# First layer of a four-layer decoder trunk on one core: VectorE's queue in another order, and the query and gate projections in turn

## The chip, the core and the metric

One core of a Trainium2 chip runs the whole program. The time is device microseconds of one execution on that core. The number of the kernel before is the median of 3 runs, 585.58 us (585.5 to 586.86). The engines are named as in the profile: PE is TensorE (matmuls; PEld its weight loads), DVE is VectorE, ACT is ScalarE, POOL is GpSimd, and SP issues most of the DMAs. Each engine takes its own instructions in order; between engines, semaphores order the work.

## The reference

The input x has 256 positions of 1024 numbers. Four layers follow each other, each `h = h + rms_norm(mixer(rms_norm(h)))`, with four different mixers. Only the first one is touched here, a sparse attention with 16 query heads in 4 groups that share keys and values:

```
q, kc, vc, ks, vs, kw, vw, gl, z = split_cols(u @ w_in, A_SPLITS)
kcmp, vcmp = compress(kc, ...), compress(vc, ...)          # 15 blocks of 32 positions
p_c = masked_softmax(q @ kcmp - slopes * dist, dist >= 0)  # compressed branch, 15 columns
p_s = masked_softmax(q @ ks  - slopes * dist, dist >= 0)   # selected branch: here all 4 blocks
p_w = masked_softmax(q @ kw  - slopes * dist, mask)        # window branch
o = gates[0] * (p_c @ vcmp) + gates[1] * (p_s @ vs) + gates[2] * (p_w @ vw)
return (o * silu(z)) @ w_out
```

With 256 positions the selected branch and the window branch see the same causal columns. The gates are sigmoids of `gl`.

## The kernel before, in words

Every float32 product with a weight matrix is made of three matmuls on fp32r halves. A weight tile is loaded as `raw` (by SP, 512 KB, five buffers), ACT makes its high half `whi` (line 129), DVE its low half `wlo` (line 72, a subtraction), and PE multiplies high by high, high by low and low by high (weights by activations, lines 222 to 224 in `mm3`). `push_proj` puts one projection of 256 columns into the queue `fq` as 16 steps of three matmuls each, and hands the finished PSUM tile `mm` (three buffers) to a function `use`.

The first layer's attention runs as 8 units (`nsa_unit`) of two query heads each, two units to a group of four heads. PE's order is that of the source (it is scheduled by hand), and in this layer DVE's too; ACT's order is chosen by the tile scheduler from priorities. `nsa_order` lists the pieces of the units: `first` and `second` of unit p (the scores of the first and of the second half of the positions), the two transpositions of unit p-1 (`trans`, line 328, into the two PSUM buffers `pt`), then `finish` (the rest of the scores) and `pvs` of unit p-1 (the products with the values, lines 344, 347 and 875). Ahead of each even unit stands `cmp_front` (scores of the compressed branch, line 783), in each odd unit `cmp_back` (their transposition, line 811). Between two pieces `fill` pops steps of waiting projections from `fq`, two at first and then one, so that PE has work while the other engines make the softmax.

What DVE does for a unit:

- `softmax` (line 321): one operation adds mask and scores, writes `P` and accumulates the maximum `mxa` (a second, short instruction reads it out). It frees the score tile `S` (two PSUM buffers), and ACT's exponential (line 323) follows. These are called the maxima here.
- `scale` (lines 849 to 859), called the weighting: reciprocal of the sums, times the gate, and eight multiplications of parts of `P`. PE's transposition of the unit (line 328) reads what they write.
- In each even unit the compressed branch: a reduction of its scores (line 787), five small operations that follow from one another (789 to 796), ACT's exponential (797), and five more (`cmp_weights`, 801 to 806).
- The low halves of weights (line 72), called by `low_parts` and by `push_proj`, and what `later` has put off: the low half of the queries (line 681), the gate's `zw` (430), its product with the output (381) and the low half of that (390). `later(n, f)` runs f once n more steps have been popped.

The order of the compressed branch and of the weighting comes from these calls:

```
cmp_front(g)   # lines 787 to 797 at once, ahead of the unit's first maxima
first()        # scores_of(0, (0, 1)), then CHALF (801 to 806), then SCALE of unit p-1
trans_first()  # for the last unit: SCALE, then its first transposition
```

The projections in `fq` are the queries of groups 1 to 3 (group 0 is done earlier) and then the four parts of z. `need(g)` pops steps until the queries of group g have been ready for six steps.

## Time and profile before

| what | value |
|---|---|
| median of 3 runs | 585.58 us (585.5 to 586.86) |
| the profiled execution, its time | 586.66 us |
| its span in the trace | 584.9 us |
| PE / DVE / ACT / POOL busy | 561.1 / 420.6 / 335.4 / 41.8 us |
| mean granted TensorE clock | 0.99 |
| scores of the first unit begin | 68.6 us of the span |
| output projection of the first layer begins | 168.3 us |

The profiled execution took 586.66 us, 1.08 us more than the median of the runs. Its span is 1.8 us shorter than its own time; that much lies around the span. Times inside the trace count from the span's start. The ends of matmuls are modelled and overlap the next ones, so a PE that is shown busy is not at its peak; its gaps are seen from the starts of its instructions and from the view of the waits. A granted clock of 1.00 stands for 2.4 GHz, 0.5 for 1.2 GHz; a stretch with a number between them had both.

### The profile page before, as it was taken

To read this page: it belongs to the slowest core of one execution; us is meant where nothing else is said; L and a number is where in the kernel's file an instruction comes from. 1 tells how busy PE (TensorE), PEld (TensorE's weight loads), DVE (VectorE), ACT (ScalarE), POOL (GpSimd) and SP (SyncE) were. 2 spreads that over 40 slices of the span, in tenths; PEclk is the share of its full clock that TensorE was granted. 3 is DMA by queue.
4 is the path that set the end of the run, shared out by engine and by line. 5 is a ranking of instruction groups with operands and counts; after the bars stand their busy time and mean duration, and the time that the engine had idled before them with its cause. 6 is when DMAs were issued, how large, how long until landed. Compare 5 with 4: busy or idle time off the path is not lost.

```text
span 584.9 us, 10456 instructions
## 1 busy us (share of the span) xinstructions
PE 561.1 (96%) x3930; PEld 498.2 (85%) x3930; DVE 420.6 (72%) x927; ACT 335.4 (57%) x719; POOL 41.8 (7%) x89
## 2 busy tenths in 40 slices
PE   7999988988899999999999999999999999999995
PEld 6997877866688789999988789999987898998984
DVE  5883788788837887777984877668648778888632
ACT  6743777787723475766752475558524755666410
POOL 1900000000100100000420100000001000000000
PEclk9999989998999999999999999999999999999999
DMA  9764632333315577444342468543525683332012
GB/s 295 254 241 165 232 111 79 108 101 106 121 24 228 180 271 269 145 146 145 109 149 104 156 232 307 162 146 115 153 99 171 226 316 124 131 114 73 2 37 72
DMA packets 27779, 90.96 MB, mean 155 GB/s; under 512 B 4560, under 2 KB 5200, under 8 KB 27728
## 3 DMA queue, kind: packets, MB, share of 16 engines
q1 hardware_dynamic: 26144, 86.09, 43.4%
q10 hardware_dynamic: 1584, 4.20, 2.2%
q8 instruction: 31, 0.51, 0.4%
q14 instruction: 20, 0.16, 0.1%
HBM read 89.22 MB, written 1.05 MB: 154 GB/s over the span
## 4 chain that ended last, share of the span: by engine, by line
PE 81%; DVE 8%; issue 4%; ACT 3%; DMA 2%; POOL 1%; POOLq 0%; DVEq 0%; ACTq 0%; SPq 0%
PE mm L222 15%; PE mm L223 14%; PE mm L224 14%; PE mm L289 6%; PE mm L288 6%; PE mm L287 6%; PE pt L328 4%; PE S L338 3%; DVE wlo L72 3%; PE o L344 2%; ACT whi L129 2%; DMA raw<-in_a_t_dram 1%; PE o L692 1%; PE pt L210 1%; PE mm L519 1%
## 5 line engine op out<-in xcount | busy, mean ns | idle before, releaser
L222 PE MATMUL mm<-uth,whi 128*128 128x256 f32 x736 | 218.6, 297 | 0.0
L72 DVE TENSOR_TENSOR wlo<-raw,whi 128x1024 fp32r<-128x1024 f32 (+1 forms) x153 | 182.0, 1205 | 41.8 <-ACT whi L129 41.3
L224 PE MATMUL mm<-uth,wlo 128*128 128x256 f32 x736 | 208.7, 284 | 2.1 <-DVE wlo L72 2.1
L223 PE MATMUL mm<-utl,whi 128*128 128x256 f32 x736 | 208.7, 284 | 0.0
L129 ACT ACTIVATE whi<-raw 128x1024 fp32r<-128x1024 f32 (+1 forms) x153 | 157.0, 1044 | 67.4 <-PE mm L223 33.4
L222 PEld LDWEIGHTS mm<-uth,whi 128*128 128x128 f32 x736 | 141.4, 192 | 14.1 <-issue 13.3
L224 PEld LDWEIGHTS mm<-uth,wlo 128*128 128x128 f32 x736 | 141.4, 192 | 2.3 <-DVE wlo L72 2.3
L223 PEld LDWEIGHTS mm<-utl,whi 128*128 128x128 f32 x736 | 141.6, 192 | 0.8
L287 PE MATMUL mm<-whi,qT 128*128 128x512 f32 x128 | 50.4, 394 | 0.0
L288 PE MATMUL mm<-whi,kT 128*128 128x512 f32 x128 | 49.9, 390 | 0.0
L289 PE MATMUL mm<-wlo,qT 128*128 128x512 f32 x128 | 49.9, 390 | 0.0
L287 PE MATMUL mm<-whi,uth 128*128 128x512 f32 (+1 forms) x112 | 42.5, 380 | 0.0
L289 PE MATMUL mm<-wlo,uth 128*128 128x512 f32 (+1 forms) x112 | 42.1, 376 | 0.0
L288 PE MATMUL mm<-whi,utl 128*128 128x512 f32 (+1 forms) x112 | 42.0, 375 | 0.0
L328 PE MATMUL pt<-ident,P 128*128 128x128 f32 x180 | 28.9, 290 | 5.9 <-DVE P L858 4.5
L321 DVE CUSTOM_DVE_ANT_0 P<-S,mask 128x128 f32<-128x128 f32 (+1 forms) x96 | 29.1, 353 | 7.2 <-PE S L834 4.9
L452 ACT ACTIVATE junk<-mm 128x512 bf16<-128x512 f32 x16 | 9.5, 595 | 42.7 <-PE mm L289 42.7
L323 ACT ACTIVATE P<-P,mxa 128x128 f32<-128x128 f32 (+1 forms) x64 | 28.4, 446 | 6.5 <-DVE mxa L321 6.5
L168 ACT ACTIVATE PT<-pt 128x384 f32<-128x384 f32 x58 | 26.1, 483 | 8.1 <-PE pt L328 7.9
L328 PEld LDWEIGHTS pt<-ident,P 128*128 128x128 f32 x180 | 21.3, 146 | 8.9 <-DVE P L858 3.5
L289 PEld LDWEIGHTS mm<-wlo,qT 128*128 128x128 f32 x128 | 24.0, 188 | 5.1
L288 PEld LDWEIGHTS mm<-whi,kT 128*128 128x128 f32 x128 | 24.1, 188 | 4.7
(207 smaller groups left out, 757.8 us busy)
## 6 DMA issues: line engine op xcount, KB each, us to landing
raw<-in_a_t_dram SPq DMA_DIRECT2D x24, 512.0 KB, 4.4
raw<-in_b_t_dram SPq DMA_DIRECT2D x24, 512.0 KB, 4.8
raw<-in_d_t_dram SPq DMA_DIRECT2D x24, 512.0 KB, 4.5
raw<-in_c_t_dram SPq DMA_DIRECT2D x20, 512.0 KB, 4.9
raw<-in_w_dram SPq DMA_DIRECT2D x8, 512.0 KB, 4.5
raw<-in_a_o_dram SPq DMA_DIRECT2D x8, 512.0 KB, 3.4
raw<-in_b_v_dram SPq DMA_DIRECT2D x8, 512.0 KB, 5.8
raw<-in_b_o_dram SPq DMA_DIRECT2D x8, 512.0 KB, 3.5
```

What stands on the lines that cost most here:

```text
L72: lo_of = (POOL if on_pool else DVE).tensor_tensor(lo, t, hi.bitcast(F32), op=OP.subtract)
L129: ACT.activation(hi, t, AF.Copy)
L168: ACT.activation(dst, src, AF.Copy)
L222: PE.matmul(o, sh, mh, start=first, stop=False)
L223: PE.matmul(o, sh, ml, start=False, stop=False)
L224: PE.matmul(o, sl, mh, start=False, stop=last)
L287: PE.matmul(o, sh, wh[:, j, c0:c1], start=k == 0, stop=False)
L288: PE.matmul(o, sl, wh[:, j, c0:c1], start=False, stop=False)
L289: PE.matmul(o, sh, wl[:, j, c0:c1], start=False, stop=k == 7)
L321: DVE.tensor_tensor_reduce(out=P[:, c0:c1], in0=S, in1=mask[:, c0:c1], scale=-slope, scalar=BIG, op0=OP.add, op1=OP.min, accum_out=mx)
L323: ACT.activation(P[:, c0:c1], P[:, c0:c1], AF.Exp, bias=mx, scale=-1.0, accum_out=l)
L328: PE.transpose(pt[:, i, :], P[:, i * 128:(i + 1) * 128], ident)
```

## The change

Five edits, all in the first layer's attention or in helpers that act otherwise only there:

- The small operations of the compressed branch become two lists of calls in `CHALF`. The first list (lines 789 to 797 of before) runs in `first`, behind the unit's first maxima, in turn with the weighting of unit p-1 (`mixed`); the second (801 to 806) runs in `second`, behind its maxima.
- `scale` returns a list of calls, which `mixed` alternates with the others. For the last unit it is called two pieces ahead of the transposition.
- The projections are pushed as queries 1, z 0, queries 2, z 1, queries 3, z 2, z 3, and the weight tiles are loaded in that order.
- `push_proj` makes the low half of the next weight tile at the first step of a tile and no longer at the third.
- The low half of the queries and the gate's `rest` are put off by 5 and 6 steps and no longer by 3. The high half of the queries gets an early priority on ACT, the gate's tanh loses its late one, and `overdue` runs whatever is due, not only the head of its list.

```diff
@@ -57,7 +57,7 @@
     add("a_t", *range(8))
     add("a_t", 8, 9)
     add("w1", *range(8), split=False)
-    add("a_t", *range(10, 24))
+    add("a_t", 10, 11, 16, 17, 12, 13, 18, 19, 14, 15, 20, 21, 22, 23)
     add("a_o", *range(8))
     for n in "bcd":
         add(n + "_v", *range(8))
@@ -88,8 +88,12 @@
             f()
 
     def overdue(everything=False):
-        while waiting and (everything or waiting[0][0] <= plan["count"]):
-            waiting.popleft()[1]()
+        due = [w for w in waiting if everything or w[0] <= plan["count"]]
+        for w in due:
+            waiting.remove(w)
+            w[1]()
+        if due:
+            overdue(everything)
 
     def advance(most=len(seq)):
         while True:
@@ -257,7 +261,7 @@
         def step(c, k):
             if c == 0 and k == 0:
                 t["o"] = ps.tile([128, 2, 256], F32, name="mm", bufs=NMM)
-            for i, at in ((idx[c], 0), (idx[c] + 1, 2)):
+            for i, at in ((idx[c], 0), (idx[c] + 1, 0)):
                 if k == at and i in low:
                     low.pop(i)()
             wh, wl = parts[idx[c]]
@@ -355,8 +359,8 @@
             self.oT = big.tile([128, 8, 256], F32, name="oT")
             self.ready = 0
 
-        def push(self):
-            for i in range(4):
+        def push(self, *which):
+            for i in which or range(4):
                 push_proj(lambda z, i=i: self.have_z(i, z))
 
         def have_z(self, i, z):
@@ -364,7 +368,7 @@
                 self.w[i] = w
                 self.go()
 
-            with tc.high_priority(offset=LATEZ):
+            with tc.high_priority(offset=0 if st["own"] else LATEZ):
                 self.silu(z, got)
 
         def have_o(self, p):
@@ -430,7 +434,7 @@
             DVE.scalar_tensor_tensor(w, w, 1.0, z, op0=OP.add, op1=OP.mult)
             got(w)
 
-        later(3, rest)
+        later(6, rest)
 
     def out_proj(g, l):
         last = l == 3
@@ -677,8 +681,9 @@
             r, other = HALF[j], HALF[1 - j]
             hs = slice(4 * g + j, 4 * g + j + 3, 2)
             hi, sc = t["q"][r, hs, :], cq[r, 2 * g:2 * g + 1]
-            ACT.activation(hi, o[r], AF.Copy, scale=sc)
-            later(3, lambda r=r, other=other, hs=hs, hi=hi, sc=sc: DVE.scalar_tensor_tensor(
+            with tc.high_priority(offset=EARLY):
+                ACT.activation(hi, o[r], AF.Copy, scale=sc)
+            later(5, lambda r=r, other=other, hs=hs, hi=hi, sc=sc: DVE.scalar_tensor_tensor(
                 t["q"][other, hs, :], o[r], sc, hi.bitcast(F32), op0=OP.mult, op1=OP.subtract))
         ready[g] = plan["count"]
 
@@ -759,8 +764,11 @@
         for f in steps[4 * q:4 * q + 4]:
             fq.append(f)
             pop()
+    ga = Gate(0.5, silu_tanh)
     for g in range(1, 4):
         push_proj(lambda o, g=g: keep_q(o, g))
+        ga.push(g - 1)
+    ga.push(3)
     for _ in range(9):
         pop()
     hidden_t()
@@ -769,8 +777,6 @@
     second_layer()
     qT = t["q"]
 
-    ga = Gate(0.5, silu_tanh)
-    ga.push()
     CS, PTC, CHALF, SCALE = {}, {}, [], []
 
     def cmp_front(g):
@@ -786,24 +792,31 @@
         two = sc[:, 0:256].rearrange("p (a s n) -> p a n s", s=2, n=16)[:, :, 0:15, :]
         DVE.tensor_reduce(out=cs.rearrange("p b a n -> p (b a) n"), in_=two, axis=AX.X, op=OP.add)
         pairs = cs.rearrange("p b (c j) n -> p (b c) j n", j=2)
-        DVE.tensor_tensor(pairs, pairs, dcmp.rearrange("p b c n -> p (b c) n")[:, :, None, :]
-                          .to_broadcast([128, 4, 2, 15]), op=OP.add)
-        DVE.tensor_tensor(cs, cs, slc[:, g, None, :, None].to_broadcast([128, 2, 4, 15]), op=OP.mult)
         cs8 = cs.rearrange("p b a n -> p (b a) n")
         cm, cl = small(8, "cm", 2), small(8, "cl", 2)
-        DVE.tensor_reduce(out=cm, in_=cs8, axis=AX.X, op=OP.max)
-        DVE.tensor_scalar(cm, cm, -1e20, None, op0=OP.max)
-        DVE.tensor_tensor(cs8, cs8, cm[:, :, None].to_broadcast([128, 8, 15]), op=OP.subtract)
-        ACT.activation(cs, cs, AF.Exp)
-        CHALF.append(lambda: cmp_weights(g, cs, cs8, cl))
-
-    def cmp_weights(g, cs, cs8, cl):
-        DVE.tensor_reduce(out=cl, in_=cs8, axis=AX.X, op=OP.add)
-        DVE.tensor_scalar(cl, cl, 1e-30, None, op0=OP.max)
-        DVE.reciprocal(cl, cl)
-        DVE.tensor_tensor(cl.rearrange("p (b a) -> p b a", b=2), cl.rearrange("p (b a) -> p b a", b=2),
-                          gate[:, :, 4 * g:4 * g + 4], op=OP.mult)
-        DVE.tensor_tensor(cs8, cs8, cl[:, :, None].to_broadcast([128, 8, 15]), op=OP.mult)
+        cl2 = cl.rearrange("p (b a) -> p b a", b=2)
+        CHALF.append([
+            lambda: DVE.tensor_tensor(pairs, pairs, dcmp.rearrange("p b c n -> p (b c) n")[:, :, None, :]
+                                      .to_broadcast([128, 4, 2, 15]), op=OP.add),
+            lambda: DVE.tensor_tensor(cs, cs, slc[:, g, None, :, None].to_broadcast([128, 2, 4, 15]), op=OP.mult),
+            lambda: DVE.tensor_reduce(out=cm, in_=cs8, axis=AX.X, op=OP.max),
+            lambda: DVE.tensor_scalar(cm, cm, -1e20, None, op0=OP.max),
+            lambda: DVE.tensor_tensor(cs8, cs8, cm[:, :, None].to_broadcast([128, 8, 15]), op=OP.subtract),
+            lambda: ACT.activation(cs, cs, AF.Exp)])
+        CHALF.append([
+            lambda: DVE.tensor_reduce(out=cl, in_=cs8, axis=AX.X, op=OP.add),
+            lambda: DVE.tensor_scalar(cl, cl, 1e-30, None, op0=OP.max),
+            lambda: DVE.reciprocal(cl, cl),
+            lambda: DVE.tensor_tensor(cl2, cl2, gate[:, :, 4 * g:4 * g + 4], op=OP.mult),
+            lambda: DVE.tensor_tensor(cs8, cs8, cl[:, :, None].to_broadcast([128, 8, 15]), op=OP.mult)])
+
+    def mixed(*lists):
+
+        lists = [deque(x) for x in lists]
+        while any(lists):
+            for x in lists:
+                if x:
+                    x.popleft()()
 
     def cmp_back(g):
         ptc = ps.tile([128, 4, 128], F32, name="pt", bufs=2)
@@ -842,21 +855,21 @@
         def finish():
             scores_of(1, (1,))
             low_parts(1)
-            SCALE.append(scale)
+            SCALE.append(scale())
 
         def scale():
             l = t["l"]
-            DVE.reciprocal(l, l)
             gv = bass.AP(tensor=gate.tensor, offset=gate.offset + 16 + 2 * p,
                          ap=[list(gate.ap[0]), [1, 2], [16, 2], [48, 2]])
-            DVE.tensor_tensor(l.rearrange("p (j r b) -> p j r b", j=2, r=2),
-                              l.rearrange("p (j r b) -> p j r b", j=2, r=2), gv, op=OP.mult)
+            l4 = l.rearrange("p (j r b) -> p j r b", j=2, r=2)
+            ops = [lambda: DVE.reciprocal(l, l), lambda: DVE.tensor_tensor(l4, l4, gv, op=OP.mult)]
             for br in range(2):
                 for j in range(2):
                     x = (j * 2 + br) * 2
-                    P = t["P"][j, br]
-                    DVE.tensor_scalar(P[:, 0:128], P[:, 0:128], l[:, x:x + 1], None, op0=OP.mult)
-                    DVE.tensor_scalar(P[:, 128:384], P[:, 128:384], l[:, x + 1:x + 2], None, op0=OP.mult)
+                    for b in range(2):
+                        P = t["P"][j, br][:, 128 * b:128 * b + 128 * (b + 1)]
+                        ops.append(lambda P=P, x=x + b: DVE.tensor_scalar(P, P, l[:, x:x + 1], None, op0=OP.mult))
+            return ops
 
         def trans(br):
             t["PT", br] = [transpose_p(t["P"][j, br], "a") for j in range(2)]
@@ -878,25 +891,20 @@
 
         def first():
             scores_of(0, (0, 1))
-            for rest in (CHALF, SCALE):
-                if rest:
-                    rest.pop()()
+            mixed(*(x.pop(0) for x in (SCALE, CHALF) if x))
 
         def second():
             scores_of(1, (0,))
+            if CHALF:
+                mixed(CHALF.pop(0))
             low_parts(1)
 
-        def trans_first():
-            if SCALE:
-                SCALE.pop()()
-            trans(0)
-
         front = [first, second, finish]
-        back = [trans_first, lambda: trans(1), pvs]
+        back = [lambda: trans(0), lambda: trans(1), pvs]
         return front, back
 
     def nsa_order():
-        units = [nsa_unit(p) for p in range(8)] + [([lambda: None] * 3, None)]
+        units = [nsa_unit(p) for p in range(8)] + [([lambda: mixed(SCALE.pop()), *[lambda: None] * 2], None)]
         order = []
         for p in range(9):
             f, b = units[p][0], units[p - 1][1] if p else [lambda: None] * 3
```

How the instructions move, at three places of DVE's queue (line numbers of the changed kernel are 4 to 14 higher; PE's queue stays the same but for which projection a step belongs to, two steps more ahead of the last group's compressed scores and two fewer later).

DVE at the start of an even unit, the third group of heads (`cs`, `cm` and `cl` belong to the compressed branch, `la` and `P` to the weighting, `mxa` to the maxima), before:

```order
L787 TENSOR_REDUCE cs<-S 128x120
L789 TENSOR_TENSOR cs<-cs,dcmp 128x120
...
L796 TENSOR_TENSOR cs<-cs,cm 128x120
L321 ISA P,mxa<-S,mask 128x128
L321 ISA mxa 128x1
...
L801 TENSOR_REDUCE cl<-cs 128x8
...
L806 TENSOR_TENSOR cs<-cs,cl 128x120
L849 RECIPROCAL la<-la 128x8
L852 TENSOR_TENSOR la<-la,gate 128x8
L858 TENSOR_SCALAR P<-P,la 128x128
```

and now:

```order
L793 TENSOR_REDUCE cs<-S 128x120
L325 ISA P,mxa<-S,mask 128x128
...
L865 RECIPROCAL la<-la 128x8
L799 TENSOR_TENSOR cs<-cs,dcmp 128x120
L865 TENSOR_TENSOR la<-la,gate 128x8
L801 TENSOR_TENSOR cs<-cs,slc 128x120
L871 TENSOR_SCALAR P<-P,la 128x128
L802 TENSOR_REDUCE cm<-cs 128x8
L871 TENSOR_SCALAR P<-P,la 128x256
...
L325 ISA P,mxa<-S,mask 128x256
...
L807 TENSOR_REDUCE cl<-cs 128x8
```

The first maxima now follow the reduction at once, the weighting alternates with the first five operations of the compressed branch, and the last five come behind the next maxima.

DVE where the units begin (`hk` and `hv`, the hidden layer of the compression, are the copies into `P` and `zw`), before:

```order
L681 SCALAR_TENSOR_TENSOR qT<-mm,cq,qT 64x2x256 x2
L719 COPY P<-pt 128x120
L722 COPY zw<-pt 128x240 x2
L72 TENSOR_TENSOR wlo<-raw,whi 128x1024
L734 SCALAR_TENSOR_TENSOR kc<-S,kc 128x4x15
L742 TENSOR_TENSOR v<-o,bm 60x256 x4
L787 TENSOR_REDUCE cs<-S 128x120
```

and now:

```order
L686 SCALAR_TENSOR_TENSOR qT<-mm,cq,qT 64x2x256 x2
L72 TENSOR_TENSOR wlo<-raw,whi 128x1024
L724 COPY P<-pt 128x120
L727 COPY zw<-pt 128x240 x2
L739 SCALAR_TENSOR_TENSOR kc<-S,kc 128x4x15
L747 TENSOR_TENSOR v<-o,bm 60x256 x4
L793 TENSOR_REDUCE cs<-S 128x120
L72 TENSOR_TENSOR wlo<-raw,whi 128x1024
L325 ISA P,mxa<-S,mask 128x128
```

One low half now runs ahead of the copies of the hidden layer, another ahead of the first maxima.

DVE at the last unit (`zw`, `oT` and `kT` belong to the gate and its halves), before:

```order
L321 ISA P,mxa<-S,mask 128x256
L321 ISA mxa 128x1
L72 TENSOR_TENSOR wlo<-raw,whi 128x1024
L430 SCALAR_TENSOR_TENSOR zw<-zw,mm 128x512
...
L381 SCALAR_TENSOR_TENSOR oT<-oT,zw 128x512
L390 TENSOR_TENSOR kT<-oT,qT 128x512 x2
L849 RECIPROCAL la<-la 128x8
...
L858 TENSOR_SCALAR P<-P,la 128x128
```

and now:

```order
L325 ISA P,mxa<-S,mask 128x256
L325 ISA mxa 128x1
L72 TENSOR_TENSOR wlo<-raw,whi 128x1024
...
L865 RECIPROCAL la<-la 128x8
L865 TENSOR_TENSOR la<-la,gate 128x8
L871 TENSOR_SCALAR P<-P,la 128x128
...
L434 SCALAR_TENSOR_TENSOR zw<-zw,mm 128x512
```

The weighting of the last unit now stands ahead of the gate's operations.

## Rows read from the trace of the kernel before

**Rows 1.** The page, part 1: busy time, share, instructions.

```profile
PE 561.1 (96%) x3930; PEld 498.2 (85%) x3930; DVE 420.6 (72%) x927; ACT 335.4 (57%) x719; POOL 41.8 (7%) x89
```

**Rows 2.** Busy time by stretch: its length, each engine, granted clock, DMA.

```profile
68.60:91.80 23.20, 19.99 (x146) 18.00 (x145) 19.32 (x66) 17.06 (x46) 0.00 (x0) 0.93 0.36 114
91.80:114.40 22.60, 21.13 (x170) 17.90 (x169) 18.76 (x72) 16.41 (x50) 0.00 (x0) 1.00 0.28 94
114.40:134.60 20.20, 17.48 (x136) 13.88 (x134) 18.05 (x70) 16.88 (x54) 0.00 (x0) 1.00 0.33 105
134.60:155.20 20.60, 17.88 (x130) 14.64 (x129) 16.98 (x71) 15.63 (x49) 1.05 (x3) 0.92 0.33 106
155.20:168.30 13.10, 11.45 (x83) 9.60 (x81) 5.43 (x20) 5.96 (x12) 0.53 (x2) 0.87 0.14 46
```

**Rows 3.** The same view, three stretches with a low granted clock.

```profile
78.00:82.00 4.00, 4.00 (x22) 3.96 (x22) 3.94 (x17) 3.15 (x10) 0.00 (x0) 0.57 0.71 217
139.00:144.00 5.00, 3.93 (x21) 3.76 (x21) 4.42 (x17) 3.17 (x8) 0.00 (x0) 0.66 0.01 3
160.00:165.00 5.00, 5.00 (x33) 3.54 (x31) 0.64 (x2) 1.19 (x3) 0.00 (x0) 0.66 0.01 2
```

**Rows 4.** Waits of PE, 68.6 to 168.3: total us, times, longest.

```profile
PE pt L328 <- DVE P L858: 4.5, 4, 1.7
PE S L833 <- DVE mxa L321: 3.5, 4, 1.1
PE mm L224 <- DVE wlo L72: 2.1, 1, 2.1
PE pt L328 <- ACT PT L168: 1.1, 3, 0.4
```

**Rows 5.** DVE timeline, unit 6: start, us, line, operation [idle before].

```profile
135.99 0.28 DVE L789 TENSOR_TENSOR cs<-cs,dcmp 128x120 f32<-128x120 f32 x1
136.31 0.28 DVE L791 TENSOR_TENSOR cs<-cs,slc 128x120 f32<-128x120 f32 x1
...
137.34 0.28 DVE L321 CUSTOM_DVE_ANT_0 P<-S,mask 128x128 f32<-128x128 f32 x1
...
137.55 0.28 DVE L321 CUSTOM_DVE_ANT_0 P<-S,mask 128x128 f32<-128x128 f32 x1
...
138.18 0.27 DVE L801 TENSOR_REDUCE cl<-cs 128x8 f32<-128x120 f32 x1
...
139.34 0.19 DVE L849 RECIPROCAL la<-la 128x8 f32<-128x8 f32 x1
...
139.77 0.29 DVE L858 TENSOR_SCALAR P<-P,la 128x128 f32<-128x128 f32 x1
```

**Rows 6.** PE timeline of unit 6, and the last transposition.

```profile
137.99 0.47 PE L833 MATMUL S<-kT,qT 128*128 128x512 f32 x1 [1.12 <-DVE mxa L321]
...
140.11 1.59 PE L328 MATMUL pt<-ident,P 128*128 128x128 f32 x6 [1.07 <-DVE P L858]
...
158.55 1.07 PE L328 MATMUL pt<-ident,P 128*128 128x128 f32 x6 [1.65 <-DVE P L858]
```

**Rows 7.** PE timeline, units 0 and 1.

```profile
72.54 0.47 PE L833 MATMUL S<-kT,qT 128*128 128x512 f32 x1 [0.77 <-DVE mxa L321]
...
77.37 0.39 PE L224 MATMUL mm<-uth,wlo 128*128 128x256 f32 x1 [2.12 <-DVE wlo L72]
```

**Rows 8.** DVE timeline, 72 to 79.

```profile
74.55 1.52 DVE L681 SCALAR_TENSOR_TENSOR qT<-mm,cq,qT 64x512 fp32r<-64x512 f32 x2
76.09 1.22 DVE L72 TENSOR_TENSOR wlo<-raw,whi 128x1024 fp32r<-128x1024 f32 x1
```

**Rows 9.** DVE timeline at the last unit.

```profile
155.13 0.68 DVE L430 SCALAR_TENSOR_TENSOR zw<-zw,mm 128x512 f32<-128x512 f32 x1
...
158.12 0.29 DVE L858 TENSOR_SCALAR P<-P,la 128x128 f32<-128x128 f32 x1
```

**Rows 10.** ACT groups by shape, 68.6 to 168.3.

```profile
L129 ACT ACTIVATE whi<-raw 128x1024 fp32r<-128x1024 f32 x18 | 19.0, 1054 | 3.2 <-DMA raw<-in_a_o_dram 1.9 <-DMA raw<-in_a_t_dram 0.7
...
L680 ACT ACTIVATE qT<-mm,cq 64x512 fp32r<-64x512 f32 x6 | 4.1, 680 | 1.3 <-PE mm L224 1.3
...
L427 ACT ACTIVATE zw<-mm 128x512 f32<-128x512 f32 x3 | 1.8, 597 | 0.1
```

## The prediction

> **What bounds the kernel now.** I read the page's busy times first: PE is shown busy for 561.1 of 584.9 us [rows 1], so on the whole the kernel is bound by TensorE, and a change on VectorE can only be worth the time in which PE waits. The change touches the first layer's attention, so the next view is the busy time by stretch, cut at the scores of each group of heads [rows 2]. From 68.6 to 168.3 us, five stretches of 23.2, 22.6, 20.2, 20.6 and 13.1 us, PE has most of its gaps, and DVE is busy for 19.3, 18.8, 18.1 and 17.0 us of the first four: the two engines hold each other up. ACT has 15.6 to 17.1 us there. Outside these 99.7 us the order of the work is unchanged, so what is won here is kept, and what is lost too.
>
> Third, who keeps PE waiting there [rows 4]: transpositions wait for weighted P, 4.5 us in four waits; scores wait for the maxima that free a score tile, 3.5 us in four; one projection waits 2.1 us for a low half of weights; transpositions wait 1.1 us for ACT to empty a `pt` buffer. Together 11.2 us. Fourth, the granted clock: three stretches stand at 0.57 to 0.66 [rows 3], each right behind one of the longest waits: 2.12 us at 77.37 [rows 7], 1.12 and 1.07 us at 137.99 and 140.11, and 1.65 us at 158.55 [rows 6]. At 1.00 less the granted share, the last two lose 5 x 0.34 = 1.7 us of full-clock time each, and the first 4 x 0.43 = 1.7 us.
>
> Last, DVE's timeline in unit 6 [rows 5] says why PE waits. Five operations of the compressed branch run from 135.99 to 137.34, then the maxima, then from 138.18 five more, and only at 139.34 the weighting. PE's wait of 1.12 us ends with the maxima and that of 1.07 us with the first weighted P [rows 6]. Nobody needs the compressed branch that early: its transposition comes a unit later.
>
> **The change, part by part.** The sum goes against the profiled execution's own 586.66 us; the median of the runs lies 1.08 us below that, and I take the gain from the median.
>
> (a) Maxima ahead of the compressed branch. They start 137.34 - 135.99 = 1.35 us earlier [rows 5], more than any of the four waits for them (at most 1.12 us). In the even units 2, 4 and 6 these waits go: 3.5 - 0.77 = 2.7 us. In unit 0 it stays: a low half now stands ahead of those maxima, 1.22 us [rows 8] in place of 1.35 us, so the 0.77 us [rows 7] is not counted. Bounds: 1.1 us (if only the wait listed at 137.99 goes) and 3.5 us. I take **-2.7 us**.
>
> (b) Weighting in units 2, 4 and 6. Five operations (138.18 to 139.34, 1.16 us [rows 5]) leave the place ahead of it. Five others come into it, one after each operation of the weighting. Operations that depend on each other start 0.32 us apart (135.99 to 136.31), independent ones of the same length 0.21 us (137.34 to 137.55) [rows 5], so a chain that alternates with another one should hide about 0.1 us at each link. From the end of the maxima to the first weighted part were 139.77 + 0.29 - 138.18 = 1.9 us; now it is a reciprocal, two small operations of the branch, the gate and one multiplication, about 0.9 us as an estimate from these spacings. PE arrives 1.1 us earlier too, and then is paced by the second and later parts, which have an operation of the branch between each two. Of the 4.5 - 1.65 = 2.85 us [rows 4, 6] I take half, **-1.4 us**; bounds 0 and 2.85 us.
>
> (c) The last weighting stood behind the gate's operations, which start at 155.13, and its first part came at 158.12 [rows 9]; PE waited 1.65 us [rows 6]. It now stands ahead of them and two filling pieces ahead of its transposition: **-1.65 us**; bounds 0.8 us (should ACT's last exponentials come late) and 1.65 us.
>
> (d) The low half for which PE waits at 77.37 stood behind the query's 1.52 us and took 1.22 us [rows 8]. It is now issued a whole tile ahead. The 2.12 us [rows 7] go, but not for nothing. The low half that now precedes the copies of the hidden layer holds up the second layer of the compression by up to 1.22 us on PE, less the time the copies took ahead of it: I take 0.7 us. And the maxima that free the score tile for unit 1 still stand behind queries 1 and a low half, so PE stops there instead, a step later. I take **-1.0 us**; bounds +1.2 us (the whole of the copies' delay, nothing won) and -2.1 us.
>
> (e) DVE's own length. Some 6 hidden links of 0.11 us in each of three groups make 18 x 0.11 = 2.0 us of DVE time, in stretches of which DVE fills 82 to 89% [rows 2]. About half should reach PE in the odd units, which wait on the maxima at the end of this queue: **-1.0 us**; bounds 0 and 2.0 us. Queries and z in turn move work and take none away. Queries 3 now come just ahead of the compressed scores of group 3. Their low half, 1.52 us, stands behind maxima and a low half of weights (0.8 + 1.22 us), 3.5 us in all, and PE has about as much to do in between (the products with the values and three steps). That cover just holds; without it, up to 1.5 us.
>
> (f) The clock. The two later stretches follow waits that (a) to (c) shorten. Of their 3.4 us [rows 3] I take half, **-1.7 us**; bounds 0 and 5.1 us (with the first).
>
> (g) Next late is ACT. With PE earlier, transpositions meet `pt` buffers that ACT has not emptied, because one whi of 1054 ns or a pair of queries of 680 ns each [rows 10] is in front. Now 1.1 us [rows 4]; I add **+1.2 us**, bounds 0 and 3 us.
>
> The sum is -2.7 - 1.4 - 1.65 - 1.0 - 1.0 - 1.7 + 1.2 = -8.25 us, about -8.3: 578.4 us against the profiled execution, and **577.3 us** for the median.
>
> **A rule that speaks against (b) and (e).** The rows say that an independent operation starts 0.21 us after one of 0.28 us, and a dependent one after 0.32 us [rows 5]. The Trainium skill, "VectorE: DVE Perf Modes", section "The DRAIN you can't avoid", says that the next operation does not start until the pipe is empty, whether or not a semaphore stands between, and its table for kernel authors advises against chaining for speed. By that rule alternating hides nothing. The trace disagrees for operations that do not wait for each other: 0.21 us is less than the operation's own length. I go by the rows.
>
> **The rivals.**
>
> DVE stays the bound (22%). Only the waits in which DVE did plainly misplaced work go: (a) and (c), 4.35 us. The rest of DVE's queue is as full as before, and PE, arriving earlier, waits for the second and later weighted parts. For it: DVE's 82 to 89% [rows 2]. Against it: DVE too has idle time, waiting for scores that PE would deliver earlier. 585.58 - 4.35 = **581.2 us**.
>
> Alternating hides nothing (6%). DVE keeps its 2.0 us in the three groups: (e) falls away and (b) loses about as much again as the links in front of the first weighted parts, 0.3 us in each unit. 577.3 + 1.0 + 0.9 = **579.2 us**. This is what the skill's section named above would have.
>
> The full clock (10%). All three slow stretches vanish and (b) comes whole: (f) is 5.1 in place of 1.7 us, (b) 2.85 in place of 1.4. 577.3 - 3.4 - 1.45 = **572.5 us**. For it: each stretch has its wait right in front. Against it: the first wait moves by a step and does not go.
>
> ACT becomes the bound, and it is slower (6%). ACT's queue holds whi, query halves and tanh ahead of the copies that empty `pt`, and the change gives the queries an early priority and the tanh no late one. If in each of the 8 units a transposition waits for one whi more (8 x 1.05 = 8.4 us), and in six for a pair of queries or a tanh (3 x 1.36 + 3 x 0.6 = 5.9 us), that is 14.3 us against 9.45 us won in (a) to (f): **590.4 us**. It decides from 9.45 / 8 = 1.2 us for each unit. For it: ACT's 17 us in the first stretches. Against it: only 1.1 us of such waits now [rows 4], and 3.3 to 6.2 us without work in each of the four stretches [rows 2].
>
> Nothing is won (6%): PE waits as long at the next operation of DVE's queue, **585.6 us**.
>
> **How the numbers follow.** The forecast has 50%: 577.3 us, with 575 to 580 us as its own range, from the middle parts of (a) to (g). A change under 0.3%, 1.76 us, can hardly be told from none here. The forecast, "DVE stays the bound", "hides nothing" and "full clock" are faster by more: 0.88. The same 0.06, slower 0.06. The range is 572 to 583 us: it takes in all four faster cases, down to the low bounds of (a) and (c), 1.9 us, with 0.7 us from the rest (583), and leaves out the last two, and the tails, about 0.17 together.
>
> **What would show it.** Right: the waits of scores for maxima fall from 3.5 us to about 1, those for weighted P from 4.5 to about 1.5, the wait of 2.1 us for a low half goes, the output projection begins at about 160 us of the span and not at 168.3, and the clock is near 1.00 in the fourth and fifth stretch. Wrong: waits of transpositions for ACT above 3 us; a new wait of the compressed scores for the low half of queries 3; or PE waiting for scores' maxima behind the five operations that moved to the second half of a unit. If the later layers change by more than 1 us, the reasoning that they only shift is wrong.

## The result, and the profile after the change

The changed kernel takes **579.28 us** (median of 4 runs, 578.36 to 579.91) against 586.22 us for the kernel before on the same chip (4 runs): a ratio of 0.9881, with a 95% interval of 0.9857 to 0.9904. It is 6.9 us faster; 8.3 us had been forecast, and the range of 572 to 583 us holds the result, as does the forecast's own range of 575 to 580. The profiled execution took 579.91 us, with a span of 578.2 us where before it was 584.9.

The page, part 1, of the kernel after. Against [rows 1] PE has 1.8 us less of busy time and DVE 2.0 us less, with as many instructions as before:

```profile
PE 559.3 (97%) x3930; PEld 495.3 (86%) x3930; DVE 418.6 (72%) x927; ACT 335.0 (58%) x719; POOL 41.9 (7%) x89
```

Busy time by stretch (length, PE, PEld, DVE, ACT, POOL, granted clock, DMA share, GB/s). The cuts answer to those of [rows 2]: the scores of the compressed branch for groups 0 to 3, the last unit, and the output projection. The last row is all that follows it:

```profile
69.50:92.05 22.55, 19.69 (x143) 17.56 (x143) 18.55 (x65) 16.61 (x48) 0.00 (x0) 0.92 0.33 113
92.05:114.30 22.25, 21.24 (x170) 17.95 (x169) 18.54 (x71) 16.58 (x51) 0.00 (x0) 1.00 0.26 92
114.30:134.05 19.75, 18.38 (x140) 14.58 (x139) 17.73 (x70) 16.62 (x51) 0.00 (x0) 1.00 0.37 111
134.05:152.20 18.15, 17.30 (x132) 13.47 (x130) 15.42 (x70) 15.47 (x48) 0.55 (x3) 1.00 0.37 118
152.20:161.50 9.30, 9.26 (x76) 7.66 (x75) 6.16 (x20) 6.20 (x14) 1.02 (x2) 1.00 0.20 63
161.50:578.20 416.70, 407.75 (x2774) 364.33 (x2773) 296.69 (x553) 224.07 (x443) 24.35 (x35) 1.00 0.46 155
```

Three things are to be seen. First, what follows the output projection lasts 416.7 us, and lasted 584.9 - 168.3 = 416.6 us: the later layers only shifted. Second, the five stretches now sum to 92.0 us and were 99.7; they begin 0.9 us later, so 6.8 us of span were won. PE's idle time in them fell from 99.7 - 87.9 = 11.8 us to 92.0 - 85.9 = 6.1 us, and its busy time from 87.9 to 85.9 us: **5.6 us less idle and 2.1 us less busy, less 0.9 us of a later start**. The work is the same, so the fall in busy time is read as slow clock that went. It need not be all of it: in the last section's pair of executions busy time shows 1.0 us of a difference of 1.6. Third, the gain is not spread out. The scores of the groups begin at 69.48, 92.07, 114.32 and 134.06 and the output projection at 161.56 us; before, at 68.60, 91.68, 114.38, 134.55 and 168.30. Groups 0, 1 and 2 became 0.4 to 0.5 us shorter each, and group 3 with the last unit 33.75 - 27.50 = 6.25 us; two steps of projections, six matmuls, moved from group 3 to group 2.

Waits of PE between 60 and 170 us (total us, times, longest), to be read against [rows 4]:

```profile
PE S L846 <- DVE mxa L325: 4.3, 5, 2.1
PE pt L332 <- ACT PT L172: 0.8, 2, 0.4
PE S L735 <- DVE P L724: 0.5, 1, 0.5
```

The 4.5 us for weighted P and the 2.1 us for a low half have gone altogether, and ACT (0.8 us) did not become a bound. But scores wait for the maxima as long as before, 4.3 us instead of 3.5, and in other places. PE's timeline in unit 1 has more than half of it (start, us, line, operation, idle time before and its releaser):

```profile
77.77 0.28 PE L847 MATMUL S<-tu,qT 128*128 128x256 f32 x1
80.18 0.36 PE L846 MATMUL S<-kT,qT 128*128 128x256 f32 x1 [2.13 <-DVE mxa L325]
...
81.74 0.77 PE L846 MATMUL S<-kT,qT 128*128 128x512 f32 x1 [0.30 <-DVE mxa L325]
```

DVE's timeline at that place says what the maxima stood behind:

```profile
75.31 0.27 DVE L807 TENSOR_REDUCE cl<-cs 128x8 f32<-128x120 f32 x1
...
76.46 1.22 DVE L72 TENSOR_TENSOR wlo<-raw,whi 128x1024 fp32r<-128x1024 f32 x1
77.71 1.51 DVE L686 SCALAR_TENSOR_TENSOR qT<-mm,cq,qT 64x512 fp32r<-64x512 f32 x2
79.26 0.42 DVE L325 CUSTOM_DVE_ANT_0 P<-S,mask 128x256 f32<-128x256 f32 x1
```

The second half of the compressed branch (75.31 to 76.46), a low half of weights, and the low half of queries 1: 79.26 - 75.31 = 3.95 us, and none of it is what PE waits for. The low half that held PE up at 77.37 before [rows 7] comes early enough now, and PE stands for 2.13 us one operation of DVE's queue later. Behind that wait comes the one stretch of slow clock that is left, 0.57, most of it at the lower of the clock's two levels (1.2 and not 2.4 GHz):

```profile
81.00:85.00 4.00, 3.70 (x19) 3.20 (x18) 3.93 (x24) 2.54 (x9) 0.00 (x0) 0.57 0.40 135
```

The two later ones of [rows 3] are gone: the fourth and fifth stretch of the table above stand at 1.00. The waits in front of them are gone too, but that these brought the slow clock is not shown: in the third experiment the waits ahead of the first of the two are still there, and the clock is 1.00. DVE's timeline in unit 6 is the change as it was meant, beside [rows 5]: maxima first, then the weighting (L865, L871) and the compressed branch (L799 to L804) in turn:

```profile
135.82 0.29 DVE L325 CUSTOM_DVE_ANT_0 P<-S,mask 128x128 f32<-128x128 f32 x1 [0.28 <-PE S L847]
...
136.67 0.20 DVE L865 RECIPROCAL la<-la 128x8 f32<-128x8 f32 x1
136.78 0.23 DVE L799 TENSOR_TENSOR cs<-cs,dcmp 128x120 f32<-128x120 f32 x1
136.93 0.17 DVE L865 TENSOR_TENSOR la<-la,gate 128x8 f32<-128x8 f32 x1
137.05 0.28 DVE L801 TENSOR_TENSOR cs<-cs,slc 128x120 f32<-128x120 f32 x1
137.25 0.28 DVE L871 TENSOR_SCALAR P<-P,la 128x128 f32<-128x128 f32 x1
```

The first weighted part starts 0.58 us after the last maxima, and 139.77 - 138.18 = 1.59 us after them before. On PE, the transpositions of unit 6 and the last one have no idle time in front, where [rows 6] have 1.07 and 1.65 us:

```profile
137.59 1.61 PE L332 MATMUL pt<-ident,P 128*128 128x128 f32 x6
...
153.74 1.07 PE L332 MATMUL pt<-ident,P 128*128 128x128 f32 x6
```

### The profile page after: what moved, and what is told of

Read it like the earlier page. It is cut to its first block, busy times and chain, and to the rows that moved or that the text cites. A ratio compares the mean times of both kernels' runs of the same rounds, so it can differ in the third digit from the quotient of the medians.

```text
span 578.2 us, 10454 instructions
## 1 busy us (share of the span) xinstructions
PE 559.3 (97%) x3930; PEld 495.3 (86%) x3930; DVE 418.6 (72%) x927; ACT 335.0 (58%) x719; POOL 41.9 (7%) x89
## 4 chain that ended last, share of the span: by engine, by line
PE 80%; DVE 9%; issue 5%; ACT 2%; POOL 1%; DMA 1%; SPq 0%; POOLq 0%; DVEq 0%; ACTq 0%
PE mm L226 15%; PE mm L227 14%; PE mm L228 14%; PE mm L293 7%; PE mm L292 7%; PE mm L291 7%; DVE wlo L72 4%; PE S L342 3%; PE pt L332 3%; PE o L348 2%; PE o L697 1%; DVE P L325 1%; PE pt L214 1%; DMA h<-in_x_dram 1%; ACT whi L133 1%
## 5 line engine op out<-in xcount | busy, mean ns | idle before, releaser
L291 PEld LDWEIGHTS mm<-whi,qT 128*128 128x128 f32 x128 | 24.1, 188 | 4.7
```

The source lines that it names most:

```text
L291: PE.matmul(o, sh, wh[:, j, c0:c1], start=k == 0, stop=False)
```

## The experiments

Two theories were set against each other. **Order**: PE waits for whatever stands ahead in DVE's queue, so what counts is which operation is first in a unit. **Load**: DVE is the engine that is full, so only the length of its work counts. Each kernel was timed beside the kernel before on the same chip; ratios are to that, with 95% intervals. All edits are to the changed kernel, unless it is said otherwise.

**1. The compressed branch's first half ahead of the maxima again**, with nothing of it left in the alternation.

```diff
             lambda: ACT.activation(cs, cs, AF.Exp)])
+        mixed(CHALF[-1])
+        CHALF[-1] = []
```

> The changed kernel with one part undone: the first five operations of the compressed branch stand ahead of the unit's first maxima again, and no longer alternate with the weighting. Theory of the order (PE waits for what stands ahead in DVE's queue): the waits of scores for maxima come back in units 2, 4 and 6, about 1.1 us each, and the weighted P comes later, so 582 to 583.5 us against 579.3. Theory of the load (DVE's amount of work sets the time, its order does not): only the 0.75 us in each of three groups that alternating had hidden come back, at most 2.2 us, without new waits for maxima: 580.5 to 581.5 us.

582.02 us, ratio 0.9936 (0.9915 to 0.9957): 2.7 us of the 6.9 go. PE waits 6.9 us in eight stops for maxima, against 4.3 in five, and the waits of the even units are back, here on PE's timeline in units 0, 2 and 6:

```profile
75.57 0.47 PE L848 MATMUL S<-kT,qT 128*128 128x512 f32 x1 [1.91 <-DVE mxa L325]
...
95.91 0.47 PE L848 MATMUL S<-kT,qT 128*128 128x512 f32 x1 [0.50 <-DVE mxa L325]
...
139.24 0.47 PE L848 MATMUL S<-kT,qT 128*128 128x512 f32 x1 [1.13 <-DVE mxa L325]
```

The last two are those of before (0.50 and 1.12 us, the latter in [rows 6]). They go with the place of the maxima, as term (a) has it. The kernel has also lost the alternation, and in unit 0 its maxima stand behind the five operations and a low half as well (1.91 us, against 0.43 after the change and 0.77 before), so its 2.7 us hold more than (a). No transposition waits for weighted P here, nor in the second experiment, though neither takes turns: what freed the weighting is that the last five operations moved behind the next maxima.

**2. The same order, without taking turns**: all of the weighting, then all of the first half.

```diff
-            mixed(*(x.pop(0) for x in (SCALE, CHALF) if x))
+            for x in (SCALE, CHALF):
+                if x:
+                    mixed(x.pop(0))
```

> The changed kernel, but the weighting runs as a whole and then the five operations of the compressed branch, not in turn. By the rows of the trace (dependent operations start 0.32 us apart, independent ones 0.21 us) the 15 operations take about 3.6 us in place of 2.86 us in units 2, 4 and 6, and the time grows by 0 to 2 us, since the first weighted parts come sooner and the later work of DVE later: 579 to 581 us. By the rule that no operation starts before the pipe is empty, the 15 operations take as long as before, 2.9 us, and the time falls a little, for the weighted parts come sooner: 578 to 579 us.

583.3 us, ratio 0.9953 (0.9936 to 0.997): 4 us of the gain go, more than either theory gave. In unit 2 the fifteen operations take 98.17 - 94.54 = 3.63 us; in turn, 97.82 - 94.96 = 2.86 us. DVE's timeline of the second experiment:

```profile
94.54 0.20 DVE L865 RECIPROCAL la<-la 128x8 f32<-128x8 f32 x1
...
96.82 0.28 DVE L799 TENSOR_TENSOR cs<-cs,dcmp 128x120 f32<-128x120 f32 x1
97.13 0.28 DVE L801 TENSOR_TENSOR cs<-cs,slc 128x120 f32<-128x120 f32 x1
...
98.17 0.42 DVE L325 CUSTOM_DVE_ANT_0 P<-S,mask 128x256 f32<-128x256 f32 x1
...
99.91 0.28 DVE L807 TENSOR_REDUCE cl<-cs 128x8 f32<-128x120 f32 x1 [0.97 <-ACT cs L805]
```

and of the kernel after, in the same unit:

```profile
94.96 0.20 DVE L865 RECIPROCAL la<-la 128x8 f32<-128x8 f32 x1
95.07 0.23 DVE L799 TENSOR_TENSOR cs<-cs,dcmp 128x120 f32<-128x120 f32 x1
...
97.82 0.41 DVE L325 CUSTOM_DVE_ANT_0 P<-S,mask 128x256 f32<-128x256 f32 x1
...
98.62 0.28 DVE L807 TENSOR_REDUCE cl<-cs 128x8 f32<-128x120 f32 x1
```

The rows show the 0.77 us, and something that neither theory had named: the chain ends later, ACT's exponential has fallen behind a `whi` and another pair of copies, and DVE stands for 0.97 us. The stretch of group 1 took 25.15 us instead of 22.25, with PE waiting 1.28 and 0.98 us in unit 3 and a clock of 0.57 behind that:

```profile
104.79 0.35 PE L846 MATMUL S<-kT,qT 128*128 128x256 f32 x1 [1.28 <-DVE mxa L325]
...
106.95 0.47 PE L846 MATMUL S<-kT,qT 128*128 128x512 f32 x1 [0.98 <-DVE mxa L325]
```

```profile
107.00:111.00 4.00, 4.00 (x20) 3.80 (x21) 3.93 (x19) 2.72 (x10) 0.00 (x0) 0.57 0.34 123
```

The eighth experiment tries to take these prices apart.

**3. The end alone**: the kernel before, with nothing but the last weighting called two pieces earlier.

```diff
-            if SCALE:
-                SCALE.pop()()
...
-        units = [nsa_unit(p) for p in range(8)] + [([lambda: None] * 3, None)]
+        units = [nsa_unit(p) for p in range(8)] + [([lambda: SCALE.pop()(), lambda: None, lambda: None], None)]
```

> The kernel before with one part of the change alone: the weighting of the last unit is called two pieces earlier, ahead of the gate's operations. Theory of the order: the wait of 1.65 us ahead of the last transposition goes, and with it the stretch of low clock behind it, 1.7 us: 582.5 to 583.5 us against 586. If the clock falls there in any case, 584.5 us. If DVE's load alone counts, no change, 586 us.

584.27 us, ratio 0.9971 (0.9948 to 0.9993); the profiled span is 581.7 us, 3.2 below that of before, all of it between the scores of group 3 and the output projection (30.12 us instead of 33.75). The waits for weighted P fall by 1.2 us and their longest is 1.1; the last transposition still waits 0.45 us. None of the later slow stretches is left in this execution:

```profile
138.42 0.47 PE L833 MATMUL S<-kT,qT 128*128 128x512 f32 x1 [1.13 <-DVE mxa L321]
...
156.83 1.07 PE L328 MATMUL pt<-ident,P 128*128 128x128 f32 x6 [0.45 <-DVE P L858]
```

The first row stands far ahead of the edit. It is the wait of [rows 6], unchanged, as is the 1.06 us of the transposition behind it; yet the clock is 1.00 from 139 to 144 us and not 0.66. So part of the 3.2 us of span can't come from the edit. By the medians the end alone is worth about 2 us (0.4 to 3.0 by the interval), less than the 2.5 to 3.5 expected; the wait is 1.2 us of it. DVE does exactly the work that it did before, which speaks for order and against load.

**4. Queries first, then the z parts**, as before the change; the rest as after.

```diff
-    add("a_t", 10, 11, 16, 17, 12, 13, 18, 19, 14, 15, 20, 21, 22, 23)
+    add("a_t", *range(10, 24))
...
-        ga.push(g - 1)
-    ga.push(3)
+    ga.push()
```

> The changed kernel with the projections and their weight tiles in the order of before (queries 1 to 3, then z 0 to 3). If taking them in turn only moves DVE's work, as predicted, the time stays within 1.5 us of 579.3: units 2 and 3 get two queries' low halves in place of one (0.8 us more there), group 3 loses the tight place ahead of its compressed scores. If it carried the gain, 583 us or more.

579.53 us, ratio 0.9894 (0.9873 to 0.9915); the span is 578.3. Waits for maxima are 4.2 us in six stops. The waits in units 3 and 5, 0.80 and 0.62 us in the changed kernel, are 0.21 and nothing here, and unit 7 has 0.38 and 0.74 us instead. Queries and z in turn move work, and are worth nothing that can be measured.

**5. The low half of the weights back at its old step.**

```diff
-            for i, at in ((idx[c], 0), (idx[c] + 1, 0)):
+            for i, at in ((idx[c], 0), (idx[c] + 1, 2)):
```

> The changed kernel with one part undone: the low half of the next weight tile is made at the third step of a tile again. It leaves the place ahead of the hidden layer's copies, so the first scores of the compressed branch should begin at about 68.6 us as before and not at 69.5, and the first maxima no longer stand behind a low half. Theory of the queue: that edit cost 0.9 us at the start, which comes back, and DVE stays without a gap through units 0 and 1, so nothing more: 578 to 578.8 us. Rival: the wait of 2.1 us for a low half comes back instead and eats it: 580 us or more.

579.52 us, ratio 0.9865 (0.9823 to 0.9906), against 579.02 us for the changed kernel beside it: no difference, and neither theory's range. The 0.53 us that PE waited for the copies at the start and the 0.43 us in unit 0 are gone, and in unit 1 PE waits 2.90 us in one stop instead of 2.13 and 0.30, for the same maxima. No wait for a low half comes back. The early low half made room for no gain that can be measured.

**6. The low half of queries 1 and 2 due thirteen steps later**, so that unit 1's maxima no longer stand behind it.

```diff
-            later(5, lambda r=r, other=other, hs=hs, hi=hi, sc=sc: DVE.scalar_tensor_tensor(
+            later(18 if g in (1, 2) else 5, lambda r=r, other=other, hs=hs, hi=hi, sc=sc: DVE.scalar_tensor_tensor(
```

> The changed kernel with the low halves of queries 1 and 2 put off by 18 steps and not 5, into stretches in which DVE idles for 1.5 to 2.5 us in units 1 and 3. Theory of the queue: PE's wait of 2.13 us for a score tile in unit 1 stands behind that 1.51 us and shrinks to about 0.5 us, the stretch of low clock behind it goes (1.7 us), and unit 3 gains up to 0.8 us: 576 to 577.5 us. If DVE's load alone counts, no change: 579.3 us. If the queries then come too late for the scores, slower: 580 us or more.

577.57 us (576.38 to 578.03), ratio 0.9836 (0.9801 to 0.9871); the span is 576.1 us. The changed kernel beside it took 578.27 to 579.92 us: all four runs here lie below its four. Waits for maxima fall from 4.3 to 1.9 us. In unit 1 the maxima follow the low half of weights at once, and PE waits 0.46 us there instead of 2.13:

```profile
78.27 1.22 DVE L72 TENSOR_TENSOR wlo<-raw,whi 128x1024 fp32r<-128x1024 f32 x1
79.40 0.42 DVE L325 CUSTOM_DVE_ANT_0 P<-S,mask 128x256 f32<-128x256 f32 x1
```

```profile
80.32 0.36 PE L846 MATMUL S<-kT,qT 128*128 128x256 f32 x1 [0.46 <-DVE mxa L325]
```

DVE's work is the same to the operation, and its order wins 1.5 us against the changed kernel's 579.02 in the same comparison. Load alone can't explain that.

**7. Both of these.**

> Both edits together: the next tile's low half at the third step, and the low halves of queries 1 and 2 put off by 18 steps. If the two act at different places of the queue, their gains add: 575 to 576.5 us. If units 0 and 1 are then bound by ACT or by the low half, as in the kernel before, no better than the late queries alone: 576 to 577.5 us.

577.04 us (576.86 to 577.66), ratio 0.9832 (0.9798 to 0.9866); the span is 575.9. This is the best version of the study: 2.0 us below the changed kernel in the same comparison and 1.7% below the kernel before. From the sixth it can't be told apart.

The changed kernel itself, a second time:

> The changed kernel once more on the same chip, so that the others are compared with it there: 579.3 us, span 578.2 us, output projection at 161.6 us.

579.02 us, ratio 0.9865 (0.983 to 0.99), as the first time; the span is 576.6 us and not 578.2, which the last section takes up. It is the measure of the fifth to seventh.

**8. The second experiment again, with ACT's exponential of group 1 ahead of the copies.**

```diff
+    def soon(cs):
+        with tc.high_priority(offset=EARLY):
+            ACT.activation(cs, cs, AF.Exp)
...
-            lambda: ACT.activation(cs, cs, AF.Exp)])
+            lambda: soon(cs)])
```

> The two lists in a row, as in the second experiment (583.3 us, its group 1 25.15 us long), with one thing moved: in group 1, ACT's exponential of the compressed branch stands ahead of the second pair of copies that empty a transposition buffer, and not behind it. VectorE's order is the same, and so are the other groups. Theory of place: VectorE stood for 0.97 us because the exponential came at 99.58; it now comes at about 98.84, the five operations behind it and the maxima of unit 3 come 0.74 us earlier, PE's waits of 1.28 and 0.98 us in unit 3 shrink by about that and the slow clock behind them goes: group 1 about 23 us, the kernel 580.5 to 582 us. Theory of length (VectorE simply has 0.77 us more to do in each of three groups, wherever ACT stands): group 1 stays above 24.5 us and the kernel at 583 us. A third outcome: the second pair of copies, 0.2 us later, holds up PE's next transposition; then a wait of transpositions for ACT appears there and the time stays or rises.

582.11 us, ratio 0.993 (0.9905 to 0.9955); the span is 579.7, against 582.0 in the second experiment. DVE now waits 0.22 us for the exponential, PE's first wait in unit 3 is 0.53 us and not 1.28, its second is as long as it was, and the slow stretch is gone:

```profile
98.94 0.28 DVE L811 TENSOR_REDUCE cl<-cs 128x8 f32<-128x120 f32 x1 [0.22 <-ACT cs L784]
```

```profile
103.82 0.36 PE L850 MATMUL S<-kT,qT 128*128 128x256 f32 x1 [0.53 <-DVE mxa L325]
...
105.98 0.47 PE L850 MATMUL S<-kT,qT 128*128 128x512 f32 x1 [0.97 <-DVE mxa L325]
```

```profile
107.00:111.00 4.00, 3.93 (x35) 3.66 (x34) 3.36 (x12) 3.60 (x12) 0.00 (x0) 1.00 0.17 68
```

Group 1 takes 23.20 us instead of 25.15. The place of the exponential is shown for 0.75 us of that, the wait that shrank. The other 1.2 us go with the slow stretch, and since one kernel with the same waits runs with and without such a stretch (last section), one profile of each can't say that the edit removed it. The kernel's 582.11 us against 583.3 don't decide it either: the two intervals overlap, and each experiment has one run at a granted clock of 0.998 or more, 582.11 us here and 581.98 there. What is left over the profile of the changed kernel, 0.95 us in group 1, 0.76 in group 2 and 0.40 in group 3 with the last unit, 2.1 us in all (the start and group 0 give 0.6 us back), is close to 3 x 0.77 = 2.3 us, the length that taking turns hides. PE's waits say the same: for maxima 0.70 us more in unit 3 than in the changed kernel, 0.71 in unit 5 and 0.73 in unit 7. Here load counts after all: DVE's queue is tight enough in these units that nearly every microsecond of it reaches PE.

Not tested by itself is the last of the five edits: the gate's `rest` put off by six steps, the priorities on ACT, and `overdue`.

## Why the prediction was right, and where it was off

**Right: the verdict, the place and most of the mechanism.** (a) The waits of the even units for maxima are gone and come back in the first experiment; unit 0 kept its own, 0.43 us. (b) The waits for weighted P went whole, 2.85 us of them in units 2, 4 and 6 where half was taken: the second and later parts, with one operation of the branch between each two, did not pace PE. The first two experiments show that the turns were not needed for it. (c) The last transposition lost its 1.65 us, and the third experiment shows 1.2 us of that by the edit alone. (f) The two later stretches of slow clock are gone from the profile; PE's busy time fell by 2.1 us in the five stretches, and 1.7 was taken. That the clock rose is borne out by more than one execution: its mean over the whole program is 0.986 to 0.995 in 33 executions of the kernel before (0.991 on the average) and 0.995 to 0.998 in the 8 of the changed one (0.996), a difference of 0.0048, which over 580 us is about 2.8 us, as an estimate. What makes it fall is not shown. The output projection begins at 161.56 us; about 160 had been written.

**Off: (d), "I take -1.0 us".** This step was mis-sized. The text had said that PE would stop a step later at the score tile of unit 1, and then priced that stop well below the wait that went. The runs show it as long: 2.13 us for 2.12, and 0.30 us more at the next tile. The cost at the start is there too: the scores of group 0 begin 0.9 us later, 0.53 us of it the wait of the second layer for its copies (0.7 was taken). The start and unit 1 together cost 0.9 + 0.3 us, less 0.3 us in unit 0: +0.9 in place of -1.0 us, a miss of 1.9 us. It follows from the trace of before alone: the low half and the queries stood one behind the other in DVE's queue [rows 8], and the maxima right behind both:

```profile
77.35 0.42 DVE L321 CUSTOM_DVE_ANT_0 P<-S,mask 128x256 f32<-128x256 f32 x1
```

To put the low half ahead of the queries changes which of them PE is waiting for, not when the last of the three is done. The fifth experiment shows no worth of this edit, the sixth that the queries were what stood in the way. The prediction had named as a sign of being wrong that PE waits for maxima behind the five operations that moved to the second half of a unit. It came, in part: they are the first 1.15 us of the queue ahead of those maxima.

**Off: (e), "-1.0 us" in the odd units.** The mechanism holds: the second and eighth experiments put the turns at some 2 us, as waits in the odd units. But the term was booked against waits that the kernel before did not have there. Its four waits for maxima stand in units 0, 2, 4 and 6, as (a) counts them; in unit 3 it was DVE that waited, for PE's scores:

```profile
105.39 0.29 DVE L321 CUSTOM_DVE_ANT_0 P<-S,mask 128x128 f32<-128x128 f32 x1 [1.26 <-PE S L834]
```

After the change it is PE that waits, in units 3 and 5 (0.80 and 0.62 us): +1.4 us in place of -1.0, a miss of 2.4 us. Without the turns they are longer by 0.7 us each (eighth experiment). With unit 1 this is why the waits for maxima did not fall from 3.5 us to about 1, as the prediction's list of signs has it, but rose to 4.3.

DVE's timeline of the kernel after, ahead of PE's new wait of 0.80 us in unit 3: two low halves and a gate product (L385) precede the maxima of the tile that PE wants:

```profile
101.03 1.51 DVE L686 SCALAR_TENSOR_TENSOR qT<-mm,cq,qT 64x512 fp32r<-64x512 f32 x2
...
103.27 1.22 DVE L72 TENSOR_TENSOR wlo<-raw,whi 128x1024 fp32r<-128x1024 f32 x1
104.41 0.68 DVE L385 SCALAR_TENSOR_TENSOR oT<-oT,zw 128x512 f32<-128x512 f32 x1
105.01 0.28 DVE L325 CUSTOM_DVE_ANT_0 P<-S,mask 128x128 f32<-128x128 f32 x1
```

**Off the other way: (g), (b) and (f).** ACT's waits were expected to grow by 1.2 us and fell by 0.3, a miss of 1.5 us; (b) gave 1.45 us more than was taken, (f) about 0.4.

**Luck in the sum.** Two misses of 4.3 us together stand against three of about 3.3. So the total was off by 8.25 - 6.7 = 1.5 us only, and its closeness says less for the terms than it seems. Not all is accounted for: the terms as measured, with 0.3 us for a transposition of the compressed branch that no longer waits for ACT, make about -7.6 us, and the span fell by 6.7; the rest lies in short gaps that the list of waits does not name.

**The rivals.** "DVE stays the bound" (581.2 us) is half right: of the waits, as many microseconds stay on DVE's maxima as there were, but the weighted P gave more than (c) alone. "Alternating hides nothing" gave 579.2 us, which is the measured time; yet its mechanism is disproved, and the agreement is chance. Fifteen operations take 2.86 us in turn and 3.63 us in a row, and the kernel loses 3 to 4 us without the turns. The Trainium skill, "VectorE: DVE Perf Modes", section "The DRAIN you can't avoid", has the next operation start only when the pipe is empty; here an operation of 0.23 us starts at 95.07, 0.11 us after one of 0.20 us, and the next independent one 0.15 us later. The trace disagrees with that rule, for operations that don't need each other's result; the section itself adds that a next operation which is not held starts earlier. ACT did not become the bound. (b) came whole, as "the full clock" had it, but the stretch in unit 1 stayed in the first profiled execution; in the second the clock was full there, with unit 1's wait unchanged, and that execution took 578.27 us and not 572.5.

## What to carry to other kernels

Before a wait is counted as won, read on in the queue of the engine that is waited for: if the next operation that the waiting engine needs stands behind the same work, the wait moves and stays as long. Put what feeds the waiting engine first, and what is needed a unit later behind it; on DVE, let two chains of short dependent operations take turns. When a chain is made longer, look also at where the other engine's next link stands in its own queue, since here a link that came 0.75 us later made PE wait 0.75 us longer. Signs and total should be read apart: here the total fitted while the waits it was made of did not.

## What had not been expected of the hardware

The same kernel with the same waits ran with and without a slow stretch. In the second profile of the changed kernel PE waits 2.13 us at the same place (80.07 us), and the clock stays at 1.00. The span is 576.6 us and not 578.2, and PE's busy time 558.3 and not 559.3 us:

```profile
80.07 0.35 PE L846 MATMUL S<-kT,qT 128*128 128x256 f32 x1 [2.13 <-DVE mxa L325]
```

```profile
81.00:85.00 4.00, 3.63 (x30) 3.37 (x29) 3.93 (x24) 3.74 (x13) 0.00 (x0) 1.00 0.37 135
```

Other executions have one at the very start, far from any edit. The sixth experiment's:

```profile
12.00:18.00 6.00, 5.64 (x31) 5.41 (x32) 5.71 (x12) 5.46 (x14) 2.07 (x5) 0.72 0.82 244
```

The first, second, fifth, sixth and seventh have this early stretch; the kernel before, both profiles of the changed one, the third, fourth and eighth don't. In those five the granted clock from 12 to 18 us is 0.72 to 0.74. At 0.72 over 6 us this is 6 x 0.28 = 1.7 us of full-clock time, and PE's first wait behind it, for the copies at L735, ends 0.7 to 2.0 us later in the first, second and sixth (68.75 to 69.66 us) than in both profiles of the changed kernel, the fourth and the eighth (67.64 to 68.08). Why the clock falls in one execution and not in the next was not settled. What follows for reading: a wait alone does not bring a slow stretch, and two single spans that differ by less than about 2 us say nothing here until their granted clocks have been compared. The best version's profile has the early stretch and still ends at 575.9 us; without it, by these figures, it would stand at 574 to 575, as an estimate.
